# Up stages of a two-layer decoder in 256-column matmuls, two weight chunks to a PSUM bank, and two buffers moved by 64 bytes

## The chip, the cores and the metric

The kernel runs on one NeuronCore of a Trainium2 chip. The metric is the device time of one execution in microseconds (us). Five engines work side by side: TensorE (PE in the profile; its weight loads are the row PEld), VectorE (DVE), ScalarE (ACT), GpSimd (POOL) and SyncE (SP), which issues the DMAs.

## What is computed

Two decoder layers run over 256 tokens of width 1024. Layer A is differential attention, layer B a block-sparse attention; each also attends into a fixed memory of 256 rows, and each ends in a squared-ReLU MLP with 4096 hidden columns:

```python
def _sq_relu_mlp(h, w_up, w_down):
    u = jax.nn.relu(h @ w_up)
    return (u * u) @ w_down
...
    for layer in range(DEPTH):
        ...
        x = x + jnp.concatenate([o_self, o_mem], axis=-1) @ a_w_out[i]
        x = x + _sq_relu_mlp(_rmsnorm(x, a_norm_mlp[i]), a_w_up[i], a_w_down[i])
    return _rmsnorm(x, final_norm)
```

The weights (24 million float32 numbers) stay in HBM and are read once. The attention needs one block only, since 256 tokens are one block.

## The kernel before

**Split products.** Every float32 operand is split into a high part that the matmul takes exactly (`float32r`) and a low part, the rest. A product is three matmuls: high by high, low by high, high by low. For a weight chunk of 128 rows by 1024 columns ScalarE makes `wh` from `w` (L336) and VectorE makes `wl = w - wh` (L338). There are 192 such chunks, streamed in one fixed order by SyncE (L313).

**Stages.** Layer A: attention products (L499), scores (L586) and their transposes, `out_proj` (L765), the MLP's up stage (L823, L827), its down stage (L871). Layer B the same, then a last part that scales and writes the output. The tokens of the MLP's input stand in the tile `xn`, shaped [128, 8, 2, 256]: for each of 8 groups `k` of 128 features the high part of 256 tokens and right behind it the low part.

**The up stage** takes 32 chunks a layer; each chunk makes 128 of the 4096 hidden columns. `wide` gives a chunk one PSUM bank of 512 columns. `hi(k)` (L823) multiplies `wh` by high and low part of `xn` at once, 512 columns, into the whole bank, for k = 0 to 7; `lo(k)` (L827) multiplies `wl` by the high part, 256 columns, into the bank's first half. So the bank ends with two halves that have to be added: ScalarE copies the second half into `u` (L786), VectorE adds the first half (L788). When both chunks of a pair are in `u`, VectorE applies relu and the tokens' norm factor `rb` (L794), ScalarE squares (L797) and splits off the high part (L809), VectorE the low part (L811), into the buffers B0 to B7. For six pairs of each layer VectorE also makes four block sums (L804 to L807).

**`out_proj`** (L765): stationary `wh` or `wl`, moving the mixed tokens, whose high and low parts are the buffers B0 and B1 (`M.O = big_tiles(0, 1)`), 256 columns to a matmul, 192 matmuls a layer. In the MLP the same eight buffers hold the hidden columns: k = 0 to 3 in B0, 4 to 7 in B1, and so on. In the down stage they are the stationary operand.

**The order.** Steps are recorded by `P.add` with an engine, an estimated duration and the keys that they read and write. `Plan.order` then plays them through: on each engine the ready step with the lowest number goes first, and buffers of limited count (4 banks `acc`, 6 `wh`, 6 `wl`, 2 `u`) are handed out on the way. The table `EARLY` shifts the number of each kind of step. A step waits for every earlier step that writes a key it names; `ps`, the bank, is such a key.

**Where buffers stand.** Tiles follow one another in SBUF. In the built program `xn` starts at byte 24928 of a partition; B0 at 200608 and B1 at 208800; the first `wh` and `wl` tiles at 79264 and 87456. Modulo 128 that is 96 for `xn` and 32 for all the others, B2 to B7 and the other `wh` and `wl` too. The rows of each tile that a matmul reads lie whole multiples of 512 bytes further on.

Of the kernel before, what the change touches and what calls it, by code (L numbers as in the profile page):

```python
# [220 lines left out]
def t_mm(n, passes=1):  # L221
    return passes * (n / 2.4 + 13.5)
# [3 lines left out]
def tile_hybrid(ctx: ExitStack, tc: tile.TileContext, xa, xb, memt, xnat, mnat, w0, wall, consts, fgain, out):  # L226
    nc = tc.nc
    const = ctx.enter_context(tc.tile_pool(name="const", bufs=1))
    ring = ctx.enter_context(tc.tile_pool(name="ring", bufs=1))
# [7 lines left out]
    P = Plan(caps, ("acc", "w", "wh", "wl", "v") + tuple(f"B{i}" for i in range(8)))  # L237
    uid = [0]

    def name(s):  # L240
        uid[0] += 1
        return f"{s}_{uid[0]}"

    def buf(cls, shape, dt=F32, pool=None):
        pool = pool or ring
        return Buf(cls, lambda slot: pool.tile(shape, dt, name=name(cls), tag=f"{cls}{slot}", bufs=1))

    def bank(cls):
        return buf(cls, [128, 512], F32, psum)
# [8 lines left out]
    def fixed(shape, nm, dt=F32):  # L258
        return const.tile(shape, dt, name=name(nm))
# [5 lines left out]
    xnt = fixed([128, KT, 2, S], "xn", F32R)  # L265
# [6 lines left out]
    rb_t = fixed([128, S], "rb")  # L272
# [46 lines left out]
    def chunk(dma_pieces=1):  # L319
        i = st_["i"]  # L320
        st_["i"] += 1
        w = buf("w", [128, CW])
        h = buf("wh", [128, CW], F32R)
        l = buf("wl", [128, CW], F32R)
        hs = (0, 1)
        if dma_pieces == 1:
            dma(lambda: w.t, wall[i], 4 * 128 * CW, w=[(w, 0), (w, 1)])
        else:
            for p in hs:
                dma(lambda p=p: w.t[:, p * 512:(p + 1) * 512], w0[p], 256 * CW, w=[(w, p)], pri=2 * p - 1.5)  # L330
        old, P.shift = P.shift, EARLY["w" + st_["layer"]]
        for p in (hs if st_["pieces"] == 2 else [hs]):
            q = p if isinstance(p, tuple) else (p,)
            sl = slice(q[0] * 512, q[-1] * 512 + 512)
            n = 512 * len(q)
            P.add(("act", t_act(n), lambda sl=sl: nc.scalar.copy(h.t[:, sl], w.t[:, sl])),  # L336
                  [(w, x) for x in q], [(h, x) for x in q])
            P.add(("dve", t_dve(n), lambda sl=sl: nc.vector.tensor_sub(l.t[:, sl], w.t[:, sl],  # L338
                                                                       h.t[:, sl].bitcast(F32))),
                  [(w, x) for x in q] + [(h, x) for x in q], [(l, x) for x in q], port=True)  # L340
        P.shift = old
        return h, l
# [15 lines left out]
    xn = Tiles(lambda k: xnt[:, k, 0], lambda k: xnt[:, k, 1], lambda k: ("xnh", k), lambda k: ("xnl", k))  # L358

    def big(i, shape, dt=F32):  # L360
        return buf(f"B{i}", shape, dt)

    def big_tiles(i, j):
        h, l = big(i, [128, KT, S], F32R), big(j, [128, KT, S], F32R)
# [6 lines left out]
    def mem_tiles(gname):  # L371
# [11 lines left out]
                early("mem")(split_scaled)(lambda w=w, i=i: w.t[:, i], [w], g[gname][:, k:k + 1], T, k)  # L383
        return T

    def rsqrt(y, ms, n):

        t = fixed([128, n], "rst")
        q = fixed([128, n], "rsq")
        nc.vector.tensor_scalar(y.bitcast(I32), ms.bitcast(I32), -0.5, float(0x5F3759DF), op0=OP.mult, op1=OP.add)  # L390
        nc.vector.tensor_mul(t, y, y)
        nc.vector.tensor_mul(t, t, ms)
        nc.vector.scalar_tensor_tensor(q, t, -10.0 / 3.0, t, op0=OP.add, op1=OP.mult)
        nc.vector.scalar_tensor_tensor(y, q, 5.0, y, op0=OP.add, op1=OP.mult)

        nc.vector.scalar_tensor_tensor(t, y, -0.5 * 0.375 ** 2, y, op0=OP.mult, op1=OP.mult)
        nc.vector.tensor_mul(t, t, ms)
        nc.vector.tensor_scalar(t, t, 0.375, 1.5 * 0.375, op0=OP.mult, op1=OP.add)
        nc.vector.tensor_mul(y, y, t)

    def rsqrt_sum(y, s):

        t = fixed([128, 1], "rst")
        nc.vector.tensor_scalar(y.bitcast(I32), s.bitcast(I32), -0.5, float(0x5F3759DF), op0=OP.mult, op1=OP.add)
        nc.vector.scalar_tensor_tensor(t, y, s, y, op0=OP.mult, op1=OP.mult)
        nc.vector.scalar_tensor_tensor(t, t, -10.0 / 3.0, t, op0=OP.add, op1=OP.mult)
# [367 lines left out]
    def mlp_up(st, sums=()):  # L774

        st.rstd()
        us = [big(i, [128, 4, 2, S], F32R) for i in range(8)]
        st_["pieces"] = 1
        first = True
        for b in range(16):  # L780
            u = buf("u", [128, 2, S])
            for mi in range(2):
                ps = bank("acc")
                wh, wl = chunk()
                wide(ps, wh, wl, lambda k: xnt[:, k], lambda k: [("xnh", k), ("xnl", k)], True, True)
                P.add(("act", t_act(S, True), lambda u=u, mi=mi, ps=ps: nc.scalar.copy(u.t[:, mi], ps.t[:, S:])),  # L786
                      [ps], [(u, mi)])
                P.add(("dve", t_dve(S), lambda u=u, mi=mi, ps=ps: nc.vector.tensor_add(  # L788
                    u.t[:, mi], u.t[:, mi], ps.t[:, :S])), [ps, (u, mi)], [(u, mi)])
            if first:  # L790
                bcast(st)
                first = False
            k0 = 2 * b % 4
            P.add(("dve", t_dve(512, True), lambda u=u: nc.vector.scalar_tensor_tensor(  # L794
                u.t, u.t, 0.0, rb_t[:, None, :].to_broadcast([128, 2, S]), op0=OP.max, op1=OP.mult)),
                [(u, 0), (u, 1), "rb"], [u], port=True)
            P.add(("act", t_act(512), lambda u=u: nc.scalar.activation(u.t, u.t, AF.Square)), [u], [u])  # L797
            if b in sums:
                dst, keys = sums[b]

                def blocks(u=u, dst=dst):
                    a = [u.t[:, k, hf * 128:hf * 128 + 128] for hf in range(2) for k in range(2)]
                    s = [dst()[:, i * 128:i * 128 + 128] for i in range(4)]
                    nc.vector.tensor_add(s[0], a[2], a[3])  # L804
                    nc.vector.tensor_sub(s[1], s[0], a[0])
                    nc.vector.tensor_sub(s[2], a[0], a[2])
                    nc.vector.tensor_sub(s[3], a[1], s[1])  # L807
                P.add(("dve", 4 * t_dve(128) + 100, blocks), [u], keys, port=True)
            P.add(("act", t_act(512), lambda u=u, t=us[b // 2], k0=k0: nc.scalar.copy(t.t[:, k0:k0 + 2, 0], u.t)),  # L809
                  [u], [(us[b // 2], b)])  # L810
            P.add(("dve", t_dve(512), lambda u=u, t=us[b // 2], k0=k0: nc.vector.tensor_sub(  # L811
                t.t[:, k0:k0 + 2, 1], u.t, t.t[:, k0:k0 + 2, 0].bitcast(F32))), [u, (us[b // 2], b)],
                [(us[b // 2], b, 1)], port=True)
        return us
# [1 line left out]
    def ukeys(us, k):  # L816
        return [(us[k // 4], k // 2), (us[k // 4], k // 2, 1)]

    def wide(ps, wh, wl, x, keys, start, stop):


        def hi(k):
            nc.tensor.matmul(ps.t, wh.t[:, k * 128:(k + 1) * 128], x(k).rearrange("p a s -> p (a s)"),  # L823
                             start=start and k == 0, stop=stop and k == 7, skip_group_check=True)

        def lo(k):
            nc.tensor.matmul(ps.t[:, 0:S], wl.t[:, k * 128:(k + 1) * 128], x(k)[:, 0],  # L827
                             start=False, stop=stop and k == 7, skip_group_check=True)
        for k in range(8):
            P.add(("pe", t_mm(512), lambda k=k: hi(k)), keys(k) + [(wh, k // 4)], [ps])  # L830
        for k in range(0, 8, 4):
            P.add(("pe", 4 * t_mm(256), lambda k=k: [lo(j) for j in range(k, k + 4)]),
                  [x for j in range(k, k + 4) for x in keys(j)] + [(wl, k // 4)], [ps])

    def block_sums():

# [565 lines left out]
```

## Time and profile before

| | us |
|---|---|
| median of 3 runs | 598.81 (598.57 to 599.1) |
| the profiled execution | 598.01 |
| its span, first to last instruction | 596.2 |
| PE busy in it | 586.0 (98%) |
| DVE busy | 506.8 (85%) |
| ACT busy | 405.5 (68%) |

The granted clock of TensorE was 0.997 of full speed over the span. Matmuls overlap in their pipeline, so the duration of one matmul in a group's row (397 ns for L823) is longer than the distance from its start to the next one's start. That distance is what a stream of matmuls costs. It is read from the chain of waits or the timeline: the pieces there give a start, a length from that start to the next piece, and a count.

### The profile page before, as it was taken

Reading aid. Unit: us, or ns where it says so; the run is one execution under the profiler, and the core shown is the slowest. Engines: PE = TensorE matmul, PEld = TensorE weight load, DVE = VectorE, ACT = ScalarE, POOL = GpSimd, SP = SyncE. Lnnn points to the kernel's source line nnn. Section 1 sums busy time; section 2 is a strip of 40 time slices with the busy share of each in tenths; the row PEclk is TensorE's granted clock in tenths of the full one; section 3 lists DMA queues with packets and bytes.
Section 4 is the critical chain, followed back from the end, with each engine's and each line's share of the span. In section 5 each row is a group of like instructions: output and inputs, shape, how many; then the busy total and the mean of one; then the engine's idle time right before and its main releaser. Section 6 shows DMA issues by size and latency. Waiting matters only on the chain.

```text
span 596.2 us, 9398 instructions
## 1 busy us (share of the span) xinstructions
PE 586.0 (98%) x3282; PEld 494.6 (83%) x3282; DVE 506.8 (85%) x937; ACT 405.5 (68%) x812; POOL 55.8 (9%) x67
## 2 busy tenths in 40 slices
PE   8999999999999999999999999999999999999995
PEld 7777878988888888888888887898888888888884
DVE  6799887789988999897988679886998889998775
ACT  6788897676766676555776579776677667665632
POOL 0131020240000000000112222000300000000002
PEclk9999999999999999999999999999999999999998
DMA  8974714335656536467477633434565555356521
GB/s 320 333 254 137 267 56 170 118 128 183 220 203 205 183 107 243 161 218 240 169 243 237 204 121 104 145 107 142 171 211 195 199 178 178 141 204 220 183 99 71
DMA packets 29999, 108.38 MB, mean 182 GB/s; under 512 B 3328, under 2 KB 3328, under 8 KB 29696
## 3 DMA queue, kind: packets, MB, share of 16 engines
q1 hardware_dynamic: 29664, 107.26, 53.3%
q8 instruction: 26, 0.43, 0.3%
q10 hardware_dynamic: 288, 0.52, 0.2%
q14 instruction: 21, 0.17, 0.1%
HBM read 106.72 MB, written 1.05 MB: 181 GB/s over the span
## 4 chain that ended last, share of the span: by engine, by line
PE 87%; DMA 4%; DVE 4%; ACT 4%; issue 1%; SPq 0%; ACTq 0%
PE t L871 22%; PE acc L823 20%; PE acc L499 15%; PE acc L827 10%; PE acc L765 7%; PE acc L871 6%; PE t L586 2%; PE t L624 2%; PE t L681 1%; DVE wl L338 1%; DMA B<-xnat 1%; DMA w<-wall 1%; ACT wh L336 1%; DMA w<-memt 1%; PE t L557 1%
## 5 line engine op out<-in xcount | busy, mean ns | idle before, releaser
L336 ACT CAST wh<-w 128x512 fp32r<-128x512 f32 (+1 forms) x232 | 182.8, 818 | 115.8 <-PE acc L823 42.6
L338 DVE TENSOR_TENSOR wl<-w,wh 128x512 fp32r<-128x512 f32 (+1 forms) x232 | 213.6, 942 | 37.2 <-ACT wh L336 36.7
L823 PE MATMUL acc<-xn,wh 128*128 128x512 f32 x512 | 131.4, 397 | 0.5 <-DVE xn L354 0.5
L871 PE MATMUL t<-wh,B 128*128 128x512 f32 (+1 forms) x368 | 111.9, 386 | 0.0
L823 PEld LDWEIGHTS acc<-xn,wh 128*128 128x128 f32 x512 | 91.3, 188 | 18.4 <-DVE xn L354 1.8
L499 PE MATMUL acc<-wh,xn 128*128 128x512 f32 x256 | 86.7, 405 | 0.5 <-ACT xn L352 0.5
L871 PEld LDWEIGHTS t<-wh,B 128*128 128x128 f32 x368 | 68.6, 188 | 13.8
L827 PEld LDWEIGHTS acc<-xn,wl 128*128 128x128 f32 x512 | 68.0, 188 | 5.5
L871 PE MATMUL t<-wl,B 128*128 128x512 f32 (+1 forms) x184 | 71.0, 386 | 0.0
L827 PE MATMUL acc<-xn,wl 128*128 128x256 f32 x512 | 69.1, 278 | 0.0
L499 PEld LDWEIGHTS acc<-wh,xn 128*128 128x128 f32 x256 | 49.0, 191 | 12.9 <-issue 1.4
L499 PE MATMUL acc<-wl,xn 128*128 128x512 f32 x128 | 51.1, 399 | 0.2 <-DVE wl L338 0.2
L765 PE MATMUL acc<-B,wh 128*128 128x256 f32 x256 | 51.0, 290 | 0.0
L452 POOL TENSOR_TENSOR sqa<-sqa,sq 128x256 f32<-128x256 f32 x21 | 20.1, 957 | 238.6 <-ACT sq L451 237.7
L765 PEld LDWEIGHTS acc<-B,wh 128*128 128x128 f32 x256 | 41.2, 191 | 0.9 <-issue 0.7
L871 PEld LDWEIGHTS t<-wl,B 128*128 128x128 f32 x184 | 34.6, 188 | 7.0
L765 PE MATMUL acc<-B,wl 128*128 128x256 f32 x128 | 36.2, 282 | 0.0
L533 POOL TENSOR_TENSOR ropet<-ropes,consts 128x256 f32<-128x256 f32 (+1 forms) x28 | 25.7, 938 | 102.5 <-ACT ropes L522 54.9
L605 ACT ACTIVATE B<-t,nm 128x128 f32<-128x128 f32 (+1 forms) x64 | 27.1, 439 | 9.0 <-DVE nm L601 5.3
L894 ACT CAST wh<-wsum 128x1024 fp32r<-128x1024 f32 x24 | 25.3, 1054 | 9.1 <-PE acc L823 3.7
L895 DVE TENSOR_TENSOR wl<-wsum,wh 128x1024 fp32r<-128x1024 f32 x24 | 28.9, 1222 | 1.9 <-ACT wh L894 1.4
L499 PEld LDWEIGHTS acc<-wl,xn 128*128 128x128 f32 x128 | 24.6, 192 | 5.1 <-DVE wl L338 0.5
(225 smaller groups left out, 892.1 us busy)
## 6 DMA issues: line engine op xcount, KB each, us to landing
w<-wall SPq DMA_DIRECT2D x191, 512.0 KB, 3.4
w<-memt SPq DMA_DIRECT2D x4, 512.0 KB, 5.5
B<-xnat SPq DMA_DIRECT2D x1, 1024.0 KB, 7.3
B<-mnat SPq DMA_DIRECT2D x1, 1024.0 KB, 9.7
xT<-xa SPq DMA_DIRECT2D x1, 540.0 KB, 3.6
w<-w SPq DMA_DIRECT2D x2, 256.0 KB, 3.3
xT<-xb SPq DMA_DIRECT2D x1, 512.0 KB, 6.3
consts<-consts SPq DMA_DIRECT2D x1, 256.5 KB, 4.5
```

What stands on the lines that cost most here:

```text
L336: P.add(("act", t_act(n), lambda sl=sl: nc.scalar.copy(h.t[:, sl], w.t[:, sl])), [(w, x) for x in q], [(h, x) for x in q])
L338: P.add(("dve", t_dve(n), lambda sl=sl: nc.vector.tensor_sub(l.t[:, sl], w.t[:, sl], h.t[:, sl].bitcast(F32))), [(w, x) for x in q] + [(h, ...
L452: P.add(("pool", t_pool(S), lambda: nc.gpsimd.tensor_tensor(self.acc.t, self.acc.t, sq.t, op=OP.add)), [sq, self.acc], [self.acc])
L499: nc.tensor.matmul(pss[hf].t[:, c0:c1], a(k)[:, ts], b.t[:, o + c0:o + c1], start=(k == 0 and i == 0), stop=(k == KT - 1 and i == 2))
L533: nc.gpsimd.tensor_tensor(t.t[:, 0:nh, e:e + 32], zs.t[:, 0:nh, 32 - e:64 - e], b(sin[:, e:e + 32]), op=OP.mult)
L605: nc.scalar.activation(p[hd].t[:, c], sp[hd].t[:, c], AF.Exp, bias=nm[hd][:, qb:qb + 1], accum_out=ss[:, hd, qb:qb + 1])
L765: nc.tensor.matmul(o, a.t[:, ws], x(k), start=(n == 0 and m % 2 == 0 and i == 0), stop=(n == KT - 1 and i == 2), skip_group_check=True)
L823: nc.tensor.matmul(ps.t, wh.t[:, k * 128:(k + 1) * 128], x(k).rearrange("p a s -> p (a s)"), start=start and k == 0, stop=stop and k == 7, ...
L827: nc.tensor.matmul(ps.t[:, 0:S], wl.t[:, k * 128:(k + 1) * 128], x(k)[:, 0], start=False, stop=stop and k == 7, skip_group_check=True)
L871: nc.tensor.matmul(ps.t[:, c0:c1], x, y, start=start and i == 0, stop=stop and i == 2, skip_group_check=True)
L894: P.add(("act", t_act(m), lambda: nc.scalar.copy(h[x].t[:, :m], src())), keys, [h[x]])
L895: P.add(("dve", t_dve(m), lambda: nc.vector.tensor_sub(l[x].t[:, :m], src(), h[x].t[:, :m].bitcast(F32))), keys + [h[x]], [l[x]], port=True)
```

## The change

Up stages: `up_chunk` takes the place of `wide`. Each chunk is 24 matmuls of 256 columns, all into one half of a bank, so that the three products are summed in PSUM; two chunks share a bank, the second in the other half. VectorE then reads the bank of two chunks directly, with relu and factor in one instruction; the copy of L786 and the add of L788 are gone. `big` makes B0 and B1 with 32 numbers more and starts them at the 16th, 64 bytes further on. `newton` lets the small reciprocal square roots share their temporaries. Nine entries of `EARLY` have other numbers.

```diff
-             scoreB=-56, ptA=128, ptB=-59, pvA=-41, pvB=145, finA=153, finB=85, evacA=38, evacB=167, prepA=148,
-             prepB=38, normA=120, normB=40)
+             scoreB=-37, ptA=136, ptB=-40, pvA=-41, pvB=145, finA=158, finB=85, evacA=55, evacB=167, prepA=154,
+             prepB=60, normA=120, normB=36)
...
     def big(i, shape, dt=F32):
-        return buf(f"B{i}", shape, dt)
+        if i > 1:
+            return buf(f"B{i}", shape, dt)
+        n = math.prod(shape[1:])
+        dims = dict(zip("abc", shape[1:]))
+        to = " ".join(dims)
+
+        def make(slot):
+            t = ring.tile([128, 2048 + 32], dt, name=name(f"B{i}"), tag=f"B{i}{slot}", bufs=1)
+            return t[:, 16:16 + n].rearrange(f"p ({to}) -> p {to}", **dims)
+        return Buf(f"B{i}", make)
...
+    def newton(n):
+        if n not in temps:
+            temps[n] = fixed([128, n], "rst"), fixed([128, n], "rsq")
+        return temps[n]
...
             u = buf("u", [128, 2, S])
+            ps = bank("acc")
             for mi in range(2):
-                ps = bank("acc")
                 wh, wl = chunk()
-                wide(ps, wh, wl, lambda k: xnt[:, k], lambda k: [("xnh", k), ("xnl", k)], True, True)
-                P.add(("act", t_act(S, True), lambda u=u, mi=mi, ps=ps: nc.scalar.copy(u.t[:, mi], ps.t[:, S:])),
-                      [ps], [(u, mi)])
-                P.add(("dve", t_dve(S), lambda u=u, mi=mi, ps=ps: nc.vector.tensor_add(
-                    u.t[:, mi], u.t[:, mi], ps.t[:, :S])), [ps, (u, mi)], [(u, mi)])
+                up_chunk(ps, mi, wh, wl)
...
             P.add(("dve", t_dve(512, True), lambda u=u, ps=ps: nc.vector.scalar_tensor_tensor(
-                u.t, u.t, 0.0, rb_t[:, None, :].to_broadcast([128, 2, S]), op0=OP.max, op1=OP.mult)),
-                [(u, 0), (u, 1), "rb"], [u], port=True)
+                u.t, ps.t.rearrange("p (a s) -> p a s", a=2), 0.0, rb_t[:, None, :].to_broadcast([128, 2, S]),
+                op0=OP.max, op1=OP.mult)), [ps, "rb"], [u])
...
+    def up_chunk(ps, mi, wh, wl):
+        o = slice(mi * S, mi * S + S)
+
+        def mm(k, w, x, **flags):
+            nc.tensor.matmul(ps.t[:, o], w.t[:, k * 128:(k + 1) * 128], xnt[:, k, x], skip_group_check=True, **flags)
 
         def hi(k):
-            nc.tensor.matmul(ps.t, wh.t[:, k * 128:(k + 1) * 128], x(k).rearrange("p a s -> p (a s)"),
-                             start=start and k == 0, stop=stop and k == 7, skip_group_check=True)
+            for x in range(2):
+                mm(k, wh, x, start=mi == k == x == 0, stop=False)
 
         def lo(k):
-            nc.tensor.matmul(ps.t[:, 0:S], wl.t[:, k * 128:(k + 1) * 128], x(k)[:, 0],
-                             start=False, stop=stop and k == 7, skip_group_check=True)
+            mm(k, wl, 0, start=False, stop=k == 7)
```

In the changed program B0 starts at byte 200224 and B1 at 208544; their contents, 64 bytes on, stand at 96 modulo 128. `xn` stays where it was. The `wh` and `wl` tiles, and B2 to B7, move down by 384 bytes, three times 128, and keep 32 modulo 128. The DMAs and GpSimd's instructions keep their order, and PE's order up to the end of layer A's `out_proj` is the same.

PE at the start of layer A's up stage, before. `acc_…` are the banks and `wh_…` the chunks' high parts, in the order of the chunks (`wh_1412` is the first chunk, `wh_1466` the second); k goes up as `xn` is finished.

```order
L823 MATMUL acc_1599<-xn_67,wh_1412 128x512 x3
L823 MATMUL acc_1612<-xn_67,wh_1466 128x512 x3
L823 MATMUL acc_1619<-xn_67,wh_1503 128x512 x3
L823 MATMUL acc_1628<-xn_67,wh_1538 128x512 x3
L823 MATMUL acc_1599<-xn_67,wh_1412 128x512
L823 MATMUL acc_1612<-xn_67,wh_1466 128x512
```

The same place in the changed program.

```order
L839 MATMUL acc_1593<-xn_67,wh_1408 128x256 x6
L839 MATMUL acc_1609<-xn_67,wh_1497 128x256 x6
L839 MATMUL acc_1619<-xn_67,wh_1562 128x256 x6
L839 MATMUL acc_1593<-xn_67,wh_1408 128x256 x2
L839 MATMUL acc_1609<-xn_67,wh_1497 128x256 x2
```

Before, four chunks take k = 0 to 2 ahead of the first matmul on k = 3; now three do, the first, third and fifth chunk, since the second shares a bank with the first and stands behind it.

DVE in the steady part of layer A's up stage, before. `u` is the pair's buffer, `wl` the low part of a chunk, `B` the hidden columns' low part.

```order
L788 TENSOR_TENSOR u_1913<-u_1913,acc_1905 128x256
L338 TENSOR_TENSOR wl_1952<-w_1832,wh_1898 128x1024
L794 SCALAR_TENSOR_TENSOR u_1913<-u_1913,rb_70 128x512
L788 TENSOR_TENSOR u_1967<-u_1967,acc_1938 128x256
L338 TENSOR_TENSOR wl_1977<-w_1889,wh_1932 128x1024
L338 TENSOR_TENSOR wl_1990<-w_1907,wh_1958 128x1024
L811 TENSOR_TENSOR B_421_1982<-u_1913,B_421_1982 128x2x256
```

The same stretch of the changed program.

```order
L338 TENSOR_TENSOR wl_2108<-w_1994,wh_2093 128x1024
L808 SCALAR_TENSOR_TENSOR u_2133<-acc_2060,rb_70 128x512
L338 TENSOR_TENSOR wl_2141<-w_2021,wh_2122 128x1024
L825 TENSOR_TENSOR B_422_2152<-u_2133,B_422_2152 128x2x256
L338 TENSOR_TENSOR wl_2173<-w_2052,wh_2160 128x1024
```

The two adds of a pair are gone, and the relu instruction reads the bank itself.

PE in layer B's attention, before: a transpose of keys or queries (L557), of probabilities (L624), one product with new weights (L499) and the first product with the memory's values (L681).

```order
L557 MATMUL t_3896<-ident_122,B_711_3577 128x128 x4
L624 MATMUL t_3904<-ident_122,B_761_3836 128x128 x4
L624 MATMUL t_3916<-ident_122,B_761_3836 128x128 x4
L557 MATMUL t_3925<-ident_122,B_711_3577 128x128 x4
L499 MATMUL acc_3931<-wh_3723,xn_67 128x512
L499 MATMUL acc_3931<-wl_3729,xn_67 128x512
L499 MATMUL acc_3931<-wh_3723,xn_67 128x512
L681 MATMUL t_3939<-B_775_3923,mv_76 64x256 x4
```

The same place in the changed program.

```order
L575 MATMUL t_4071<-ident_122,B_685_3743 128x128 x4
L642 MATMUL t_4081<-ident_122,B_734_3992 128x128 x4
L642 MATMUL t_4092<-ident_122,B_734_3992 128x128 x4
L575 MATMUL t_4099<-ident_122,B_685_3743 128x128 x4
L642 MATMUL t_4105<-ident_122,B_734_3992 128x128 x4
L699 MATMUL t_4114<-B_752_4097,mv_76 64x256 x4
```

The next transpose of probabilities now follows at once, and the product with new weights comes after the scores. Layer B's attention has a dozen such moves; no instruction is added or dropped there.

More of the change, by code (lines that the diff above doesn't have):

```diff
@@ L32 @@
 EARLY = {k + l: 0 for k in KINDS for l in "AB"}
-EARLY.update(wA=40, wB=-21, memA=20, memB=31, natA=25, natB=64, statA=-44, statB=-119, ropeA=-90, ropeB=9, scoreA=-92,
-             scoreB=-56, ptA=128, ptB=-59, pvA=-41, pvB=145, finA=153, finB=85, evacA=38, evacB=167, prepA=148,
-             prepB=38, normA=120, normB=40)
+EARLY.update(wA=40, wB=-21, memA=20, memB=31, natA=25, natB=64, statA=-44, statB=-115, ropeA=-90, ropeB=9, scoreA=-92,
+             scoreB=-37, ptA=136, ptB=-40, pvA=-41, pvB=145, finA=158, finB=85, evacA=55, evacB=167, prepA=154,
+             prepB=60, normA=120, normB=36)
 LOOK = 100
@@ L384, in mem_tiles @@
         return T
+    temps = {}
+    def newton(n):
+        if n not in temps:
+            temps[n] = fixed([128, n], "rst"), fixed([128, n], "rsq")
+        return temps[n]
     def rsqrt(y, ms, n):
-        t = fixed([128, n], "rst")
-        q = fixed([128, n], "rsq")
+        t, q = newton(n)
         nc.vector.tensor_scalar(y.bitcast(I32), ms.bitcast(I32), -0.5, float(0x5F3759DF), op0=OP.mult, op1=OP.add)
@@ L401, in rsqrt_sum @@
     def rsqrt_sum(y, s):
-        t = fixed([128, 1], "rst")
+        t = newton(1)[0]
         nc.vector.tensor_scalar(y.bitcast(I32), s.bitcast(I32), -0.5, float(0x5F3759DF), op0=OP.mult, op1=OP.add)
@@ L793, in mlp_up @@
             k0 = 2 * b % 4
-            P.add(("dve", t_dve(512, True), lambda u=u: nc.vector.scalar_tensor_tensor(
-                u.t, u.t, 0.0, rb_t[:, None, :].to_broadcast([128, 2, S]), op0=OP.max, op1=OP.mult)),
-                [(u, 0), (u, 1), "rb"], [u], port=True)
+            P.add(("dve", t_dve(512, True), lambda u=u, ps=ps: nc.vector.scalar_tensor_tensor(
+                u.t, ps.t.rearrange("p (a s) -> p a s", a=2), 0.0, rb_t[:, None, :].to_broadcast([128, 2, S]),
+                op0=OP.max, op1=OP.mult)), [ps, "rb"], [u])
             P.add(("act", t_act(512), lambda u=u: nc.scalar.activation(u.t, u.t, AF.Square)), [u], [u])
@@ L817, in ukeys @@
         return [(us[k // 4], k // 2), (us[k // 4], k // 2, 1)]
-    def wide(ps, wh, wl, x, keys, start, stop):
+    def up_chunk(ps, mi, wh, wl):
+        o = slice(mi * S, mi * S + S)
+        def mm(k, w, x, **flags):
+            nc.tensor.matmul(ps.t[:, o], w.t[:, k * 128:(k + 1) * 128], xnt[:, k, x], skip_group_check=True, **flags)
         def hi(k):
-            nc.tensor.matmul(ps.t, wh.t[:, k * 128:(k + 1) * 128], x(k).rearrange("p a s -> p (a s)"),
-                             start=start and k == 0, stop=stop and k == 7, skip_group_check=True)
+            for x in range(2):
+                mm(k, wh, x, start=mi == k == x == 0, stop=False)
         def lo(k):
-            nc.tensor.matmul(ps.t[:, 0:S], wl.t[:, k * 128:(k + 1) * 128], x(k)[:, 0],
-                             start=False, stop=stop and k == 7, skip_group_check=True)
+            mm(k, wl, 0, start=False, stop=k == 7)
         for k in range(8):
-            P.add(("pe", t_mm(512), lambda k=k: hi(k)), keys(k) + [(wh, k // 4)], [ps])
+            P.add(("pe", 228, lambda k=k: hi(k)), [("xnh", k), ("xnl", k), (wh, k // 4)], [ps])
         for k in range(0, 8, 4):
-            P.add(("pe", 4 * t_mm(256), lambda k=k: [lo(j) for j in range(k, k + 4)]),
-                  [x for j in range(k, k + 4) for x in keys(j)] + [(wl, k // 4)], [ps])
+            P.add(("pe", 456, lambda k=k: [lo(j) for j in range(k, k + 4)]),
+                  [("xnh", j) for j in range(k, k + 4)] + [(wl, k // 4)], [ps])
     def block_sums():
```

## Prediction

> **What bounds the kernel now.** I read the page's busy times and its chain of waits first, then the busy time by stage, then the chain piece by piece in the two stages that the change touches.
>
> ```profile
> span 596.2 us, 9398 instructions
> PE 586.0 (98%) x3282; PEld 494.6 (83%) x3282; DVE 506.8 (85%) x937; ACT 405.5 (68%) x812; POOL 55.8 (9%) x67
> PE 87%; DMA 4%; DVE 4%; ACT 4%; issue 1%; SPq 0%; ACTq 0%
> ```
>
> PE is busy for 586 of 596 us and carries 87% of the chain. The stages, columns PE, weight loads, DVE, ACT, POOL, clock, DMA:
>
> ```profile
> 101.20:124.05 22.85, 22.85 (x195) 22.85 (x194) 16.82 (x45) 15.68 (x45) 3.35 (x4) 1.00 0.42 139
> 124.05:212.00 87.95, 87.46 (x507) 75.83 (x506) 81.27 (x144) 60.98 (x103) 6.91 (x7) 1.00 0.56 186
> 289.15:381.30 92.15, 92.15 (x494) 74.74 (x492) 77.45 (x157) 67.07 (x156) 19.36 (x23) 1.00 0.55 178
> 414.00:503.00 89.00, 89.00 (x522) 77.43 (x521) 80.68 (x144) 62.44 (x107) 7.11 (x7) 1.00 0.56 184
> ...
> ACT wh L336 <- PE acc L823: 42.6, 45, 2.2
> ```
>
> The first row is layer A's `out_proj`, the second and fourth the up stages, the third layer B's attention. PE never rests in them but for 0.5 us; DVE has 81 of 88 us to do in an up stage, yet is not late: the last row, from the list of waits, says that ACT waited 42.6 us in all for PE to give back a `wh` buffer, so the splits run ahead of PE. Work taken from DVE and ACT here is therefore worth nothing by itself. What counts is the distance from one matmul to the next. The chain in the steady up stage (start, length, piece):
>
> ```profile
> 152.97 0.91 PE acc L827 x8
> 153.88 1.86 PE acc L823 x8
> ...
> 166.84 0.91 PE acc L827 x8
> ```
>
> Eight 512-column matmuls take 1.86 us, 232.5 ns each; eight of 256 columns take 0.91 us, 113.8 ns each. From 152.97 to 166.84 five chunks pass, 2.774 us each. Two matmuls of 256 columns (227.5 ns) are 5 ns cheaper than one of 512 on the same `xn`. But 256 columns do not cost the same everywhere:
>
> ```profile
> 109.40 5.03 PE acc L765 x42
> 381.53 2.87 PE acc L765 x24
> 587.18 2.17 PE acc L871 x18
> 265.37 6.12 PE t L871 x27
> 273.53 2.06 PE acc L871 x9
> ```
>
> `out_proj` takes 5.03/42 = 119.8 and 2.87/24 = 119.6 ns a matmul of 256 columns, the last 256-column matmuls of the down stage (moving `wh`, stationary B) 120.6. A 512-column matmul takes 226.7 ns with B stationary and 228.9 with `xn` stationary. So there are two paces at 256 columns, 114 and 120. What goes with them is the place of the buffers: at 120 the moving and the stationary operand both start at 32 modulo 128; at 114 the moving one, `xn`, starts at 96. That is a correlation of one tile, not a proof; it carries both main terms.
>
> **The change, part by part.** The counts:
>
> ```profile
> L823 PE MATMUL acc<-xn,wh 128*128 128x512 f32 x512 | 131.4, 397 | 0.5 <-DVE xn L354 0.5
> L827 PE MATMUL acc<-xn,wl 128*128 128x256 f32 x512 | 69.1, 278 | 0.0
> L765 PE MATMUL acc<-B,wh 128*128 128x256 f32 x256 | 51.0, 290 | 0.0
> L765 PE MATMUL acc<-B,wl 128*128 128x256 f32 x128 | 36.2, 282 | 0.0
> ```
>
> *Up stages:* 512 matmuls of 512 columns become 1024 of 256; with the 512 low ones, 24 to a chunk and 64 chunks. At L827's pace a chunk takes 24 x 0.1138 = 2.73 us. I take 2.74, since a few of the short pieces in the chain last 0.92, and it is 2.774 now: 0.035 x 64 = **-2.2 us**. The new matmuls have L827's tiles and alignment, and differ in that half of them read the low part, 1024 bytes on. The bounds are the two rows at 256 columns: 113.8 ns gives -2.8, 119.8 ns gives 24 x 0.1198 = 2.875, +6.5 us.
>
> *64 bytes:* the 384 matmuls of `out_proj` would go from 119.7 to 113.8 ns, -2.3 us. The last 18 of layer A gain nothing (they are beside the DVE chain below), so **-2.2 us**; bounds 0 and -2.3.
>
> The Trainium skill, page "SBUF — State Buffer", section "Specifications (TRN2)", gives SBUF lines of 16 bytes with a penalty at each crossing. 64 bytes are four such lines, so by that rule alone the shift would be worth nothing. The rows at 114 and 120 ns speak of something that this rule does not cover.
>
> *The same buffers as stationary operand:* B0 and B1 hold 8 of the 32 groups of hidden columns, by the loops 66 matmuls of 512 columns a layer, 132. They then stand to `wh` as `xn` does in 273.53's row: 132 x 2.2 ns = **+0.3 us**; bound, L823's 232.5, +0.8.
>
> *DVE and ACT* lose 64 copies and 64 adds, and one instruction reads PSUM instead of SBUF:
>
> ```profile
> L788 DVE TENSOR_TENSOR u<-u,acc 128x256 f32<-128x256 f32 x64 | 25.9, 416 | 0.7 <-ACT u L786 0.7
> L786 ACT COPY u<-acc 128x256 f32<-128x256 f32 x64 | 22.9, 363 | 1.6 <-PE acc L827 0.9 <-DVE B L811 0.7
> L794 DVE SCALAR_TENSOR_TENSOR u<-u,rb 128x512 f32<-128x512 f32 x32 | 21.8, 687 | 0.3
> L565 DVE TENSOR_TENSOR ql<-t,qh 128x512 fp32r<-128x512 f32 x8 | 5.4, 685 | 0.2
> ```
>
> The only 512-column read of a bank with two operands, L565, takes 685 ns, as L794 does from SBUF, so the relu stays at 0.69 us. 26 us of DVE and 23 of ACT go. PE hides them today: 0. A bank, though, is now held for two chunks and until the relu, which needs the norm factor `rb`:
>
> ```profile
> 140.01 0.42 DVE L481 COPY rb<-t 128x256 f32<-128x256 f32 x1
> ```
>
> `rb` is there at 140.4, 16 us after the stage's first matmul; four banks hold eight chunks, 22 us. PE waits for a bank only if `rb` comes 5 us later than that; ahead of it on DVE stand one split more (1.2) and four adds less (1.7). In the steady part a relu stands behind one split of 1.2 us, against the 5.5 us of the next pair. So 0; if this cover went, PE would stand for what DVE is late, one split of 1.2 us a layer.
>
> *The start of layer A's up stage:*
>
> ```profile
> 124.05 3.12 PE L823 MATMUL acc<-xn,wh 128*128 128x512 f32 x12
> 125.99 1.22 DVE L338 TENSOR_TENSOR wl<-w,wh 128x1024 fp32r<-128x1024 f32 x1
> 127.13 3.04 DVE L354 SCALAR_TENSOR_TENSOR xn<-xT,xn 128x256 fp32r<-128x256 f32 x5
> 127.66 3.54 PE L823 MATMUL acc<-xn,wh 128*128 128x512 f32 x14 [0.49 <-DVE xn L354]
> ```
>
> PE does twelve matmuls (four chunks, k = 0 to 2), then waits for DVE, which does adds, a split and only then `xn` for k = 3. DVE's order here is unchanged, but PE now has three chunks to fill the time, not four: 3 x 0.23 = 0.7 us of work is done later while PE stands. 0.05 comes back behind it, where PE is again held by `xn` at 0.61 us a group. **+0.65 us**; bounds 0 and +0.8. In layer B three chunks are open before and after: 0.
>
> *Order in layer B's attention.* A change between kinds of work costs PE a gap of about 0.08: in the timeline of layer A's `out_proj`
>
> ```profile
> 107.78 0.36 PE L765 MATMUL acc<-B,wh 128*128 128x256 f32 x1
> 107.98 0.28 PE L765 MATMUL acc<-B,wl 128*128 128x256 f32 x1
> ```
>
> the first matmul behind a transpose takes 0.20 us to the next start, not 0.12. By the order of instructions there are 102 such changes from layer B's first product to its up stage, and 98 in the new order: -0.3. Against it stands that a moved step can meet data that is not there yet; today the stage's row shows PE busy for all its 92.15 us. I take 0, bounds -0.5 and +1.5.
>
> *The other matmuls:* `wh` moves by 384 bytes against `xn`. Modulo 128 nothing changes; if a larger unit counts, the attention's matmuls with `xn` stationary could go from 228.9 to 226.7 or 232.5 ns:
>
> ```profile
> L499 PE MATMUL acc<-wh,xn 128*128 128x512 f32 x256 | 86.7, 405 | 0.5 <-ACT xn L352 0.5
> L499 PE MATMUL acc<-wl,xn 128*128 128x512 f32 x128 | 51.1, 399 | 0.2 <-DVE wl L338 0.2
> ```
>
> 384 of them: -0.8 to +1.4. I take 0.
>
> **Sum:** -2.2 - 2.2 + 0.3 + 0.65 = -3.45 us. The profiled execution took 598.01 (span 596.2), so 594.6 for it. It lies 0.8 below the median of the three runs, 598.81, to which the prediction refers: 598.81 - 3.45 = **595.4 us**.
>
> **The rivals.**
>
> *A, more matmuls cost more, slower.* A 256-column matmul carries a fixed cost and takes 119.8 ns wherever the stream is long; L827's 113.8 holds for runs of eight behind 512-column matmuls with their longer time to load weights. For it: two of the three kinds of 256-column streams run at 120. Against it: L827's eight show no drift within 0.91 us, run after run. Price: +6.5 up, 0 in `out_proj`, +0.3 and +0.65: 606.3. It decides from 2.774/24 = 115.6 ns on: above that pace the up stages lose.
>
> The Trainium skill names such a cost: "TensorE: Matmul & The Clock Gate", section "Back-to-back issue gap", gives N/2.4 + 2.5 ns. By it two of 256 columns cost 2.5 ns more than one of 512, an estimate of +1.3 us over 512 pairs. The rows here, 227.5 against 232.5 ns, say the reverse.
>
> *B, the 64 bytes do nothing:* `xn`'s pace has another cause, and `out_proj` stays at 119.7. Then -2.2 + 0.65 = -1.55: 597.3. For it: only one tile stands at 96, so the cause may be the tile.
>
> *C, half the gain:* reads of the low part, or the changed distance of 384 bytes, put the streams near 117 ns: up 24 x 0.117 = 2.808, +2.2; `out_proj` -1.0; +0.95: 601.0.
>
> *D, more gain:* 113.5 ns everywhere, layer B's attention 0.5 shorter, no loss at the start: -3.2 - 2.3 + 0.3 - 0.5: 593.1.
>
> **Chances.** Forecast (594.0 to 596.8) 0.52, D 0.08, B 0.14, C 0.11, A 0.15. The range 593.0 to 602.0 takes in all but A and a little of D. A measurement of this kernel tells about 0.2%, 1.2 us, from no change: faster means under 597.6, slower over 600.0. The forecast, D and somewhat over half of B are faster: 0.68. The rest of B is the same, with a little from C and the forecast's far edge: 0.10. Most of C and A are slower: 0.22.
>
> **What would show it.** Right: pieces of 16 and 8 matmuls at 1.82 and 0.91 us in the chain of the up stage, 87.5 us for 32 chunks; `out_proj` at 114 ns a matmul; PE's wait for DVE's `xn` near 127 us about 0.7 longer; the down stage 0.15 longer a layer. Wrong: a pace over 115.6 ns in the up stage, `out_proj` still at 120, attention products off 229 ns, or a wait of PE for ACT or DVE in layer B's attention that is not there today.

## The result, and the profile after

The changed kernel takes **604.72 us** (median of 4 runs, 604.66 to 608.15) against 598.91 for the kernel before (4 runs, 598.57 to 599.1). The ratio is 1.0102, with a 95% interval of 1.0079 to 1.0126: slower by 1%, where 595.4 was forecast, and outside the range of 593.0 to 602.0. The profiled execution took 604.66, its span is 602.8, at a granted clock of 0.998.

The page of the changed kernel, its span, its busy times and the shares of the chain by engine:

```profile
span 602.8 us, 10368 instructions
PE 592.0 (98%) x3794; PEld 520.6 (86%) x3794; DVE 486.2 (81%) x871; ACT 390.6 (65%) x750; POOL 56.0 (9%) x67
PE 93%; DMA 2%; ACT 2%; DVE 2%; issue 0%; SPq 0%; ACTq 0%
```

DVE lost 21 us and ACT 15, less than the 26 and 23 of the instructions that went, and PE, the bound, has 6 us more to do. The stages, each from its first matmul to the first one of the next (down B to its last matmul), in us (e1, e11 and e12 are experiments below):

| stage | before | after | e1 split alone | e11 no pads | e12 e11 + 384 bytes |
|---|---|---|---|---|---|
| attention A | 88.47 | 89.37 | 88.94 | 90.06 | 89.60 |
| out_proj A | 30.20 | 29.89 | 30.22 | 30.23 | 30.20 |
| up A | 90.69 | 92.85 | 89.69 | 92.55 | 89.68 |
| down A | 82.70 | 83.53 | 82.70 | 83.16 | 82.70 |
| attention B | 83.85 | 84.47 | 83.83 | 84.47 | 83.90 |
| out_proj B | 32.70 | 32.64 | 32.90 | 32.96 | 32.92 |
| up B | 91.82 | 93.41 | 90.51 | 93.38 | 90.28 |
| down B | 83.25 | 84.00 | 83.25 | 83.74 | 83.25 |

Both up stages became longer instead of shorter. The chain of waits of the changed kernel in them shows why (start, length, piece and count):

```profile
128.41 7.69 PE acc L839 x63
136.09 0.34 PE t L478 x4
136.43 4.58 PE acc L839 x38
141.01 0.44 PE t L497 x4
141.46 75.15 PE acc L839 x638
...
435.51 73.50 PE acc L839 x624
```

Behind the four matmuls that broadcast the norm's factor (`t L497`) each up stage is one stream of over 620 matmuls without a break: 75.15/638 = 117.8 ns and 73.50/624 = 117.8 ns from one start to the next. The forecast had 113.8, and 115.6 as the point from which the split loses. PE waits for nothing in these streams. Nor is it the granted clock, which is 1.00 (the third number from the end) in layer A's up stage before and after:

```profile
124.05:214.74 90.69, 90.20 (x523) 78.21 (x522) 83.67 (x148) 63.31 (x107) 6.91 (x7) 1.00 0.56 186
124.77:217.62 92.85, 91.80 (x779) 91.47 (x778) 74.17 (x117) 55.58 (x76) 7.09 (x7) 1.00 0.56 182
```

So most of the loss in these stages is the pace.

Two more of the forecast's signs, the groups and the timeline of PE at the start of layer A's up stage:

```profile
L839 PE MATMUL acc<-xn,wh 128*128 128x256 f32 x1024 | 132.4, 280 | 1.1 <-DVE xn L354 1.1
L808 DVE SCALAR_TENSOR_TENSOR u<-acc,rb 128x512 f32<-128x512 f32 x32 | 21.9, 690 | 27.4 <-PE acc L839 27.4
```

```profile
125.78 1.57 PE L839 MATMUL acc<-xn,wh 128*128 128x256 f32 x12
128.41 0.97 PE L839 MATMUL acc<-xn,wh 128*128 128x256 f32 x6 [1.05 <-DVE xn L354]
```

The relu that reads the bank takes 690 ns (0.69 us forecast) and now waits for PE, so DVE is not late. PE's wait for `xn` is 1.05 us where it was 0.49.

### The profile page after: what moved, and what is told of

It reads as the page before. It is cut to its first block, busy times and chain, and to the rows that moved or that the text cites. A ratio compares the mean times of both kernels' runs of the same rounds, so it can differ in the third digit from the quotient of the medians.

```text
span 602.8 us, 10368 instructions
## 1 busy us (share of the span) xinstructions
PE 592.0 (98%) x3794; PEld 520.6 (86%) x3794; DVE 486.2 (81%) x871; ACT 390.6 (65%) x750; POOL 56.0 (9%) x67
## 3 DMA queue, kind: packets, MB, share of 16 engines
HBM read 106.72 MB, written 1.05 MB: 179 GB/s over the span
## 4 chain that ended last, share of the span: by engine, by line
PE 93%; DMA 2%; ACT 2%; DVE 2%; issue 0%; SPq 0%; ACTq 0%
PE acc L839 30%; PE t L889 22%; PE acc L517 20%; PE acc L783 7%; PE acc L889 6%; PE t L604 2%; PE t L642 2%; PE t L699 1%; DMA B<-xnat 1%; PE t L575 1%; DMA xT<-xa 1%; ACT wh L336 1%; DMA w<-wall 1%; DVE wl L338 1%; DVE xT L769 0%
## 5 line engine op out<-in xcount | busy, mean ns | idle before, releaser
L839 PE MATMUL acc<-xn,wh 128*128 128x256 f32 x1024 | 132.4, 280 | 1.1 <-DVE xn L354 1.1
L839 PEld LDWEIGHTS acc<-xn,wh 128*128 128x128 f32 x1024 | 125.5, 188 | 1.6 <-DVE xn L354 1.4
L889 PE MATMUL t<-wh,B 128*128 128x512 f32 (+1 forms) x368 | 112.5, 387 | 0.0
L517 PE MATMUL acc<-wh,xn 128*128 128x512 f32 x256 | 87.1, 408 | 0.7 <-ACT xn L352 0.6
L889 PEld LDWEIGHTS t<-wh,B 128*128 128x128 f32 x368 | 68.6, 188 | 14.5
L889 PE MATMUL t<-wl,B 128*128 128x512 f32 (+1 forms) x184 | 71.3, 388 | 0.0
L839 PE MATMUL acc<-xn,wl 128*128 128x256 f32 x512 | 71.1, 280 | 0.0
L839 PEld LDWEIGHTS acc<-xn,wl 128*128 128x128 f32 x512 | 64.9, 188 | 0.0
L517 PEld LDWEIGHTS acc<-wh,xn 128*128 128x128 f32 x256 | 49.0, 192 | 14.1 <-issue 1.4
L517 PE MATMUL acc<-wl,xn 128*128 128x512 f32 x128 | 51.4, 401 | 0.2 <-DVE wl L338 0.2
L808 DVE SCALAR_TENSOR_TENSOR u<-acc,rb 128x512 f32<-128x512 f32 x32 | 21.9, 690 | 27.4 <-PE acc L839 27.4
L889 PEld LDWEIGHTS t<-wl,B 128*128 128x128 f32 x184 | 34.6, 188 | 7.2
L811 ACT ACTIVATE u<-u 128x512 f32<-128x512 f32 x32 | 20.2, 633 | 16.8 <-DVE u L808 16.6
```

The source lines that it names most:

```text
L517: nc.tensor.matmul(pss[hf].t[:, c0:c1], a(k)[:, ts], b.t[:, o + c0:o + c1], start=(k == 0 and i == 0), stop=(k == KT - 1 and i == 2))
L808: P.add(("dve", t_dve(512, True), lambda u=u, ps=ps: nc.vector.scalar_tensor_tensor(u.t, ps.t.rearrange("p (a s) -> p a s", a=2), 0.0, rb_ ...
L839: nc.tensor.matmul(ps.t[:, o], w.t[:, k * 128:(k + 1) * 128], xnt[:, k, x], skip_group_check=True, **flags)
L889: nc.tensor.matmul(ps.t[:, c0:c1], x, y, start=start and i == 0, stop=stop and i == 2, skip_group_check=True)
```

## Experiments

Each was run on one chip beside the kernel before, whose median there lay between 598.5 and 599.9; ratios are against those runs. In all of them **distance** is the byte at which the moving operand of a matmul starts, less the byte at which the stationary operand of the next matmul starts, modulo 512. Sharing the temporaries had moved every weight tile down by 384 bytes and left `xn` in place: in the up stages the distance went from 448 to 320. At first there were two theories: the **distance** sets the pace, or the **length** of the stream does (rival A: 114 ns only for runs of eight behind wide matmuls).

### e1: the split alone

```diff
-        if i > 1:
-            return buf(f"B{i}", shape, dt)
...
+        return buf(f"B{i}", shape, dt)
...
-        t, q = newton(n)
+        t = fixed([128, n], "rst")
+        q = fixed([128, n], "rsq")
...
```

> The changed kernel without the 64 bytes and without the shared temporaries: the up stages in 256-column matmuls and the new order stay, and every tile stands where it stood before (xn 448 bytes ahead of wh, modulo 512). Theory 'distance' (the pace of a 256-column matmul depends on the distance modulo 512 between what the matmul reads and what the next weight load reads; sharing the temporaries moved all of wh and wl by 384 bytes against xn and so changed it): the up stage runs at 113.7 ns a matmul, attention products with xn stationary at 229 ns, and the time is 598.9 - 2.5 + 0.5 for the start of layer A's up stage = 596.9 us. Rival 'length' (my rival A: 113.7 ns holds only for runs of eight behind 512-column matmuls): the up stage stays at 117.8 ns, and the time is about 603 us.

597.28 us (10 runs, 596.35 to 599.52), ratio 0.997, interval 0.9956 to 0.9985. The chain in layer B's up stage (`t L481` is the broadcast):

```profile
425.72 4.82 PE acc L823 x40
430.54 0.44 PE t L481 x4
430.98 73.46 PE acc L823 x648
```

648 matmuls in one stream at 113.4 ns: length is not the cause, and the split by itself does what was forecast (both up stages together 2.3 us shorter, the longer start included).

### e2: the shared temporaries alone

```diff
-        t = fixed([128, n], "rst")
-        q = fixed([128, n], "rsq")
+        t, q = newton(n)
...
```

> The kernel before with the shared temporaries alone: wh and wl 384 bytes further down, xn where it was; same instructions in the same order. Distance: the low matmuls of the up stage go from 113.7 to 117.8 ns (+2.1 us), the 528 matmuls of 512 columns with xn stationary from 229.4 to 233.2 (+2.0), the 512-column ones of the up stage stay within 2 ns: about 603 us. Length: nothing moves, 598.9 us.

600.10 (10 runs), ratio 1.0015, interval 1.0002 to 1.0028: slower, by less than expected. The chain, where L830 is the wide matmul and L834 the narrow one:

```profile
185.14 1.83 PE acc L830 x8
186.96 0.94 PE acc L834 x8
187.91 1.83 PE acc L830 x8
189.74 0.91 PE acc L834 x8
190.65 1.83 PE acc L830 x8
192.48 0.94 PE acc L834 x8
```

Two misses are in these rows. The wide matmuls became cheaper, 1.83/8 = 228.8 ns where they took 232.5. And the narrow ones run at two paces in turn, 0.94/8 = 117.5 and 0.91/8 = 113.8 ns, at one and the same distance. I noted the second and did not yet see what it meant.

### e3: a table of distances

Streams of 24 narrow and 12 wide matmuls on one tile, ahead of the kernel of before, the moving operand 32 bytes further on each time:

```diff
+    for _ in range(24): nc.tensor.matmul(wu[:, 0:256], pb[:, 1024:1152], pb[:, 0:256], start=True, stop=True)
+    for _ in range(24): nc.tensor.matmul(wu[:, 0:256], pb[:, 1024:1152], pb[:, 8:264], start=True, stop=True)
...
```

> The kernel before with streams of 24 equal matmuls of 256 columns put at its start, one stream for each distance between moving and stationary operand from 0 to 480 bytes in steps of 32, then four streams with both operands 64 bytes further on, then eight streams of 12 matmuls of 512 columns at distances 0 to 448; 74 us more in all, results unchanged. Distance: 119.5 ns at 0, 117.7 at 64, 116.0 at 192, 117.8 at 320, 113.7 at 448, from the third to the last of each stream, and the same with both moved by 64. Length: 118 to 120 ns in every stream, or 114 in the first eight and more after them.

The chain through the probes; L292 has distance 64, L296 192, L298 256, L300 320 and L304 448, L309 again 448 with both operands 64 bytes on, L311 and L313 are wide ones at 64 and 192:

```profile
11.61 2.83 PE wu L292 x24
...
22.98 2.73 PE wu L296 x24
...
28.54 2.87 PE wu L298 x24
...
34.24 2.83 PE wu L300 x24
...
45.61 2.73 PE wu L304 x24
...
59.60 2.73 PE wu L309 x24
...
65.08 2.76 PE wu L311 x12
...
70.63 2.79 PE wu L313 x12
```

The settled paces of narrow matmuls, start to start over the last twelve steps of a stream: 113.3 ns at 192 and 448; 120.0 at 0 (there the last four steps), 96, 256 and 352; 117.5 to 118.8 at the other ten. Wide ones, over the last six, take 226.7 at 0, 228.8 at 64, 232.5 at 128, 233.3 at 192. The second half of the table repeats the first: in these streams the period is 256 bytes, not 128. Moving both operands by 64 bytes changes nothing. The forecast's "modulo 128" is refuted by two rows, 64 and 192, which differ by 128 and run at 117.8 and 113.3. One expected value is off: 116.0 at 192.

### e4, e5 and e6: back to a good distance, by 128 bytes

If the distance alone decides, 128 unused bytes behind `xn` (distance 192) mend the changed kernel (e4), and one pad of 192 bytes in B0 brings B0, and B1 behind it, to 192 too (e5). e6 is e5 with the old table `EARLY`.

```diff
+    fixed([128, 32], "pad")
...
-        if i > 1:
+        if i > 0:
...
-            t = ring.tile([128, 2048 + 32], dt, name=name(f"B{i}"), tag=f"B{i}{slot}", bufs=1)
-            return t[:, 16:16 + n].rearrange(f"p ({to}) -> p {to}", **dims)
+            t = ring.tile([128, 2048 + 48], dt, name=name(f"B{i}"), tag=f"B{i}{slot}", bufs=1)
+            return t[:, 48:48 + n].rearrange(f"p ({to}) -> p {to}", **dims)
```

> The changed kernel with one unused tile of 128 bytes behind xn, so that xn stands 192 bytes ahead of wh modulo 256 again; the same instructions in the same order. Theory 'distance, period 256' (113.4 ns at 192, 117.8 at 64, 120 at 0): the up stage goes from 117.8 to 113.7 ns a matmul (1536 of them, -6.3 us), the 528 matmuls with xn stationary from 233.2 to 229.4 ns (-2.0): 604.7 - 8.3 = 596.4 us. Rival: the changed kernel is slower for another reason too (bank held longer, new order), and the time stays above 600.

> The same with B0 and B1 both 192 bytes ahead of wh modulo 256 (in the changed kernel B0 stands at 64 and B1 at 192). Distance: out_proj from 117.4 to 113.5 ns (384 matmuls, -1.5 us), the down stage's 132 matmuls with B0 or B1 stationary from 232.5 to 229 ns (-0.4): 1.9 us under the run with the pad alone, 594.5 us. Rival: out_proj waits for something else and stays where it is; then only the down stage gains.

> The run with all at 192, with the table EARLY of the kernel before. If the nine numbers matter, layer B's attention and the first up matmuls differ by 1 us or more, and so does the time; if they do not, within 0.5 us of the run before it.

| | us, runs | ratio, interval |
|---|---|---|
| e4 | 602.84 (601.68 to 604.12, 7) | 1.0051 (1.0031 to 1.0072) |
| e5 | 600.33 (598.81 to 603.22, 12) | 1.0015 (0.9999 to 1.0031) |
| e6 | 602.45 (600.16 to 603.42, 12) | 1.0044 (1.0028 to 1.0059) |

The first two were forecast 6 us too fast: the theory of distance alone falls. What takes its place stands in the chain of e5, whose two layers run the same stage at the same distance (`t L498` is the broadcast):

```profile
140.12 0.44 PE t L498 x4
140.56 71.49 PE acc L840 x607
...
432.73 0.44 PE t L498 x4
433.17 66.88 PE acc L840 x590
```

71.49/607 = 117.8 ns in layer A, 66.88/590 = 113.4 in layer B. Within one layer, the chain of e4 (`t L479` is the sum of squares, `t L498` the broadcast):

```profile
128.98 7.42 PE acc L840 x63
136.41 0.34 PE t L479 x4
136.74 4.58 PE acc L840 x38
141.33 0.44 PE t L498 x4
...
141.77 74.32 PE acc L840 x631
```

The 63 matmuls at the top take 7.42 us where the changed kernel needs 7.69: they run in the fast pace. Behind the sum of squares 38 take 4.58, as in the changed kernel, and behind the broadcast it is 117.8 ns to the end; layer B's long stream goes the same way in this trace. In e6's trace both layers are slow, which is nearly all of its loss against e5's trace: up B 93.25 against 90.62 us, while the spans differ by 2.8. Layer B's attention, which the table reorders, takes 83.86 in e5 and 83.87 in e6. Had I looked at the two times only, I would have credited the new table with 2 us. Whether the table makes the slow pace more frequent over the twelve runs of each, one trace of each cannot show.

So the new theory, **two holds**: at one distance a stream of narrow matmuls can run at 113.4 or at 117.8 ns; it keeps this pace, its hold, until something interrupts it, and the interruption decides the next one. It stood in e1's rows already: the 40 matmuls ahead of the broadcast run at 117.7 ns from start to start, the 648 behind it at 113.4.

### e7: what sets the hold

Streams of 16 narrow matmuls at four distances, each behind one of eleven interruptions:

```diff
...
+    def wide_run(d, n):
+        for _ in range(n):
+            nc.tensor.matmul(wu, pb[:, 1024:1152], pb[:, d // 4:d // 4 + 512], start=True, stop=True)
+    def fp32_run():
+        nc.tensor.matmul(wu[:, 0:128], ones, ones, start=True, stop=True)
+    def pause(n):
+        nc.scalar.copy(po[:, 0:n], wu[:, 0:n])
...
+    wide_run(448, 8); stream(448)
+    wide_run(448, 1); stream(448)
+    fp32_run(); stream(448)
+    pause(8); stream(448)
```

> Probe streams of 16 matmuls of 256 columns ahead of the kernel of before; only their paces count, the output is the reference's. Each stream has one distance (448, 192, 320 or 64 bytes) and comes behind one interruption: eight 512-column matmuls, one, a small fp32 matmul, or a pause of the engine that a read of its bank by ScalarE sets, in eight lengths. Theory 'distance alone': all eleven streams at one distance settle at one pace, 113.4 ns at 448 and 192, 117.8 at 320 and 64. Theory 'two holds': at 448 and 192 a stream can run at 113.4 or at 117.5 to 118 ns for all of its length, and the interruption ahead of it decides; then at least two of the eleven at one of these distances stay near 118 and at least two near 113.4. At 320 and 64 it expects 118 behind the pauses.

The chain through the first streams, at 448 (L298 wide, L295 narrow, L300 fp32):

```profile
10.48 1.87 PE wu L298 x8
12.36 1.83 PE wu L295 x16
14.18 0.23 PE wu L298
14.41 1.89 PE wu L295 x16
16.30 0.22 PE wu L300 x2
16.52 1.86 PE wu L295 x16
```

Behind eight wide matmuls the stream settles at 113.4; behind one it stays at 118 for its whole length (1.89); behind the fp32 one it starts at 118 and settles at 113.4 after four. Settled paces of the eleven streams at each distance: at 448 and at 192 ten at 113.4 and one, the one behind a single wide matmul, at 118; at 320 one at 113.4 (behind fp32) and ten at 118; at 64 all at 118. The number that I had asked for, two on each side, was not reached; but one distance gives two paces at 448, 192 and 320, and they last. In these probes the distance sets the odds.

### e8, e9 and e10: a pause behind the broadcast

Behind a pause eight of eight streams went to 113.4 at 448 and at 192, none of eight at 320. So PE was made to pause once in each layer, right behind the broadcast, at distance 192 (e8, on e4), 320 (e9, on the changed kernel) and 448 (e10, on e1):

```diff
...
+            if len(due) == 2:
+                due.clear()
+                nc.scalar.copy(warm, ps.t[:, 0:1])
             nc.tensor.matmul(ps.t[:, o], w.t[:, k * 128:(k + 1) * 128], xnt[:, k, x], skip_group_check=True, **flags)
```

> As e4 (the changed kernel with 128 unused bytes that bring the distance of the up stages back to 192), and in each layer TensorE pauses once right behind the broadcast of the norm's factor: ScalarE first copies one column of the bank that is being summed into an unused element. Theory 'two holds': the long run of 256-column matmuls behind the broadcast was held at 117.5 ns in both layers of e4, and a pause puts it at 113.4; some 650 matmuls in each of two layers by 4 ns is 5.3 us, less 0.4 to 0.8 us for each pause: about 598.6 us. Theory 'distance alone, and the pad itself costs': no gain, 603 to 604.5.

> The changed kernel with the same pause in each layer and nothing else; the distance of its up stages is 320. In the probes at 320 and 64 bytes 21 of 22 streams ran at 118 ns, 15 of 16 of them behind pauses or nothing but wide matmuls. Theory 'the distance decides which pace can be had, the interruption only chooses at 192': still near 117.8, so 604.7 plus 0.8 to 1.6 for the pauses, about 605.9. Theory 'the interruption alone decides': both layers at 113.4, about 600.5.

(Of the sixteen pauses at 320 and 64 all led to 118, one more than this says; the one fast stream stood behind the fp32 matmul.)

> The split alone (e1) with the pause of e8 in each layer. e1's own runs went from 596.4 to 599.5, median 597.3, and its trace ran both long runs of matmuls at 113.4 ns. Theory 'a pause ends in the fast hold at 448, as eight of eight did in the probes': 597.3 plus 0.8 to 1.6 for the two pauses, about 598.3, spread no wider than 3 us. Theory 'a pause only draws the hold anew': each layer may fall into 118 ns for 2.7 us, runs from 597.5 to 603.5, median near 600.

| | us, 12 runs each | ratio, interval |
|---|---|---|
| e8 | 602.18 (597.6 to 607.19) | 1.002 (0.9995 to 1.0044) |
| e9 | 602.62 (600.11 to 604.88) | 1.0054 (1.0033 to 1.0074) |
| e10 | 599.54 (596.7 to 604.3) | 1.0005 (0.9982 to 1.0028) |

No pause makes the good hold certain. Of e9, at the distance of the changed kernel, the two layers behind the broadcast:

```profile
144.31 55.73 PE acc L844 x491
...
435.42 64.62 PE acc L844 x548
```

113.5 ns in layer A, 117.9 in layer B: the changed kernel's own distance admits the fast hold. Of e10, at the distance of before:

```profile
141.24 70.86 PE acc L828 x601
...
433.96 66.05 PE acc L828 x582
```

117.9 in layer A, 113.5 in layer B: the slow hold is there at the distance that e1 ran fast. In e8's trace both layers run at 117.8. e8 and e9 met neither of their two forecasts; e10 came out as the one for a hold that is drawn anew. Its runs, and e8's without the longest, spread over 7 to 8 us, e9's over 4.8; each layer that is held slow costs 2.6 to 2.9. But the kernel before spread over 4.3 and 3.3 us beside them, so the spread alone proves no new draw in each run, and only one run of each has a trace. The probes with a pause did not carry over to the kernel: what in an interruption picks the hold was not found.

### e11 and e12: the pads, and 384 unused bytes

e11 is the changed kernel without the 64 bytes of B0 and B1. e12 is e11 with 384 unused bytes behind the constants, so that weights and token buffers lie where they lay before, with the same instructions in the same order:

```diff
-        if i > 1:
-            return buf(f"B{i}", shape, dt)
...
+        return buf(f"B{i}", shape, dt)
...
+    fixed([128, 96], "pad")
```

> The changed kernel without the 64 bytes in the two mixed-token buffers: the split and the shared temporaries stay. By the paces by distance: up stages as in the changed kernel (117.8); the out projections back at 119.5 from 117.4 ns (by the stages +0.4 us); the down stages' matmuls ahead of these two buffers back at 227 from 231.5 to 233.4 (by the stages -1.6 us). About 603.5 us. If the 64 bytes were worth the 2.2 us of the prediction: 606.9.

> e11 (split and shared temporaries, no pads, 604.7) with 384 unused bytes behind the last of the fixed constants that are laid out ahead of the stages, so that every weight and token buffer lies where it lay before the change, distance 448; the same instructions in the same order as e11. If the place of the weights against the normalised tokens is what the shared temporaries cost: about 597.3, as e1. If sharing the temporaries costs by itself, by new waits on VectorE: 602 to 604.7.

e11 takes 604.72 (603.97 to 607.28, 6 runs), ratio 1.0084 (1.0061 to 1.0108); e12 takes **596.90** (596.14 to 600.7, 9 runs), ratio 0.9973 (0.9955 to 0.9991). 384 bytes that nobody reads are worth 7.8 us by the medians, 1.1% by the ratios. (e11 was expected at 603.5: without the pads the down stages gained 0.6 us and not 1.6, and `out_proj` lost as much.) The chain of e11 in the steady part of layer A's up stage:

```profile
142.19 57.83 PE acc L828 x491
```

The same place in e12:

```profile
141.62 70.39 PE acc L829 x621
```

117.8 against 113.3 ns. By the table of stages the up stages give 6.0 us of it and the attention and down stages 2.0.

The traces of all runs with the split, two layers each, tell how often the long stream behind the broadcast was held fast (113.3 to 113.4 ns; all others ran at 117.8):

| distance | no pause | with a pause |
|---|---|---|
| 448 | 4 of 4 (e1, e12) | 1 of 2 (e10) |
| 320 | 0 of 4 (changed kernel, e11) | 1 of 2 (e9) |
| 192 | 1 of 6 (e4, e5, e6) | 0 of 2 (e8) |

448 and 192 are alike in the probes and not here, so the table of distances does not say which hold the kernel falls into. Without a pause the times agree at 448 and 320: the 19 runs of e1 and e12 lie between 596.14 and 600.7, the ten of the changed kernel and e11 between 603.97 and 608.15.

e12 beats the kernel before by 0.3%; it is the change without its pads, with the sharing's gain in space given up again.

## Why the prediction was wrong, step by step

**Up stages, -2.2 forecast.** The arithmetic was right and the pace was not. At 113.4 ns (e1, e12) the two stages are 2.3 and 2.6 us shorter, the longer start included. At 117.8 they cost 64 x (24 x 0.1178 - 2.774) = +3.4. The failed step is "The new matmuls have L827's tiles and alignment", with "Modulo 128 nothing changes" for the 384 bytes. The forecast had two paces and one tile that explained them by its place modulo 128; e3 shows that the distance of two operands counts, with a period of 256. It went from 448 to 320, and e11 against e12 shows what that cost in the kernel. "I take 0", with bounds of -0.8 to +1.4, was set for the attention alone; the same 384 bytes lay under the main term, where the only bound was the row at 119.8 ns. The +3.4 lies within that bound of +6.5, but the range left it to rival A.

The second half of that step is that L827's pace was taken for a property of the matmul. It was a pace that stood behind eight wide matmuls every 2.77 us; in e7 a stream settles at 113.4 behind eight of them and stays at 118 behind one. The split takes these entries away, and what the broadcast leaves holds for 70 us. At 448 that cost nothing (e1, e12). At 320, e2 with the wide matmuls has the narrow ones at 113.8 and 117.5 in turn, the changed kernel at 117.8 throughout. Rival A had seen the runs of eight, "L827's 113.8 holds for runs of eight behind 512-column matmuls", but gave length and weight loads as the cause, and e1's 648 matmuls refute these. Its time, 606.3, came nearest, by luck: it has 119.8 ns in the up stages and nothing for the other matmuls. Rival C had named "the changed distance of 384 bytes" and a pace near 117, but its 601.0 left the other stages unpriced and gave `out_proj` 1 us.

The section "Back-to-back issue gap" of the Trainium skill's page "TensorE: Matmul & The Clock Gate" gives its figures by the column count. Its N/2.4 + 2.5, which it gives for a matmul by itself and not for a stream, makes an estimate of 109.2 ns for 256 columns; the rows here have 113.3 to 120 for one and the same shape, so what decided this case lies outside the rule.

**64 bytes, -2.2 forecast, -0.7 found.** Against e11, `out_proj` is 0.34 and 0.32 us shorter. The data of B0 came to distance 64 and those of B1, whose start also moves by B0's pad, to 192; of the three matmuls of a product one stays at 119.5 ns from start to start (B0, ahead of `wl`), one goes to 117.7 (B0, ahead of `wh`) and one to 116.0 (B1). None comes to 113.8.

**B0 and B1 as stationary operand, +0.3 forecast, +0.6 found** (down A 0.37, down B 0.26 against e11): about 231 to 233.5 ns for the wide matmuls ahead of them, close to the upper bound. With the line before, the 64 bytes are worth nothing: 604.72 with and without.

**Other matmuls, 0 forecast, +2.0 found.** Those with `xn` stationary (384 in L517, 108 in L889) went from distance 64 to 192 and take about 233.3 ns for 229.5, 1.9 us in all; e3 has 228.8 and 233.3 at these distances, and e11 is 2.0 us longer than e12 in the attention and down stages.

**Start of layer A's up stage, +0.65 forecast:** PE's wait grew by 0.56 us. Right.

**DVE, ACT and the bank that is held longer, 0:** right; DVE waits for PE in L808's row. **Order in layer B's attention, 0:** right; e12, which has the new order, spends 83.90 us there, 83.85 before.

The terms as found: +3.4 + 0.45 (the start of layer A's up stage, from start to start) - 0.7 + 0.6 + 2.0 = +5.8. The medians differ by 5.8, but the terms come from the traces, whose spans differ by 6.6: 0.8 us is not assigned. Some of it may be `out_proj` of layer B, which is 0.2 longer in e1, e11 and e12 than before, though its matmuls and their distances are the same there.

## What to carry to other kernels

Before a pace is carried over to a longer stream, look at what stands ahead of it and whether the two buffers keep their distance; freeing a few hundred bytes elsewhere moves every tile that is laid out behind, and here cost more than the split that it came with gained. When a pace is read from short runs, ask what restarts them. And where a kernel's runs spread by more than an edit is worth, read the pace of each stage from the trace before crediting the edit.

## What was not expected of the hardware

In e3's streams the start-to-start time of float32r matmuls depended on the distance between the moving operand and the next stationary one with a period of 256 bytes: 113.3 to 120.0 ns for 256 columns, 226.7 to 233.3 for 512. And at one distance (448, 320, 192) a stream ran at either 113.4 or 117.8 ns for as long as 600 matmuls, without any wait in the trace, until the next interruption; why a stream enters one or the other stays open.
